# Branch A's logits: the product of the high parts in 64 rows of TensorE, two heads side by side, and the cross terms in 128 rows

## The chip, the cores and the metric

The kernel runs on one core of a Trainium2 chip. The metric is the device time of one execution in microseconds (us). Before the change three executions gave 1948.72, 1949.85 and 1950.54 us; the median is 1949.85 us. The execution that the profiler recorded took 1953.81 us, of which 1952.0 us lie between its first and its last instruction (the span).

The engines are named as in the profile: PE is TensorE (matrix products), PEld its weight loads, DVE is VectorE, ACT is ScalarE, POOL is GpSimd, SP is the queue that issues the DMAs.

## The reference

One encoder block over 2048 tokens of width 1024. An input projection feeds two attention mixers, A and B, whose outputs are gated, projected, merged and added to the residual. The change concerns the logits of mixer A, a window of 128 tokens to either side with 8 query heads of width 64 that share 2 key heads:

```python
qa = head_rms_norm(qa.reshape(bsz, S, A_Q_HEADS, HEAD_DIM), q_norm_a[layer]) * scale
ka = head_rms_norm(ka.reshape(bsz, S, A_KV_HEADS, HEAD_DIM), k_norm_a[layer])
...
scores = jnp.einsum('bnqkgd,bnmkd->bkgnqm', qb, kw).astype(jnp.float32)
...
logits = jnp.where(valid, scores + bias, NEG_INF)
```

Here a block of 128 queries meets the three blocks of 128 keys around it (two at either end of the sequence).

## The kernel before

**Numbers in two parts.** Products run in float16. An operand that needs more precision is split into a high part (the value rounded to float16) and a low part (what the rounding left, as float16). A product of two such operands is taken as high times high plus the cross terms high times low and low times high.

**Units.** The first part of the program works through 14 units, each a set of heads. Unit 0 and unit 2 belong to mixer A (4 query heads and 1 key head each), the other twelve to mixer B (2 heads each, one dilation). A unit has 8 pairs (`Pair`), each of which projects two blocks of 128 tokens onto the unit's query, key and value columns: 48 matmuls of line 632, in float16, into the tile `pj`. What a pair leaves in PSUM then goes through a chain of steps, among them `scale` (DVE, L692), `gain` (POOL, L699), `hi` (ACT, L705: the high parts of all normalised heads into the tile `spl`), `lo` (DVE, L709: the low parts), `swap` (POOL, L714: a copy of the key heads with their two parts exchanged) and `turn` (L722: one DMA transpose for each block, issued by SP, into the tile `kq`).

**The layout of `kq`.** `spl` holds for each token a list of slots of 128 columns, and each slot is one head: 64 columns of high parts, then 64 of low parts. After the transpose a slot has its 128 numbers over the 128 partitions, and so over the 128 rows of TensorE: high parts in partitions 0 to 63, low parts in 64 to 127. For a unit of A slots 0 to 3 are the query heads, slot 4 the key head (high over low) and slot 5 the same key head exchanged (low over high).

**Items.** An `Item` is one block of 128 queries with two heads (`h0` is 0 or 2 in A, so a block has two items). A unit of A has 32 items: 28 with three blocks of keys, 4 with two. In `logits` (L767) an item of A takes two of the three PSUM tiles `s`, one for each head, and for each head and each block of keys runs two matmuls in all 128 rows with the query slot as weights: against slot 4 (high times high and low times low, summed over the rows) and against slot 5 (both cross terms). That is 12 matmuls for three blocks of keys and 8 for two, each with its own weight load, each 128 columns wide. Then follow `maxima` (DVE, L797, one instruction for each head, which reads that head's `s` tile and takes the row's extreme value into `nmA`), `exps` (ACT, L805), `hi` (ACT, L810) and `lo` (DVE, L814) of the probabilities `p`, their DMA transpose into `pt` (L820) and `values` (PE, L831: 18 or 12 matmuls of 65 or 64 columns into `pv`).

**What sets the order.** The order on each engine is written by the program itself. `at` puts a step into a heap with a planned time, `until` emits whatever is due, and the main loop (L1077 on) emits the matmuls of line 632 one after another, with due steps between them. Planned times count in pairs; those of an item lie at fixed lags from its start (`LAGS`, `LV`), and items of A start a quarter of a pair apart. So in PE's queue an item's logits are one block of 12 matmuls among those of line 632, and the `values` of an older item follow a few matmuls later. Engines run their queues in order and wait for each other by semaphores.

Of the kernel before, what the change touches and what calls it, by code (L numbers as in the profile page):

```python
# [24 lines left out]
AF = mybir.ActivationFunctionType  # L25
OP = mybir.AluOpType
# [72 lines left out]
def block_kernel(tc, x, w_units, w_gate, w_mrg, w_out, w_bra, w_brk, gain, qkg, sink, bias_a, bias_b, b_merge, out):  # L99
    nc = tc.nc  # L100
    V = nc.vector
    A = nc.scalar
    G = nc.gpsimd
    T = nc.tensor
# [396 lines left out]
    def scale_time(t):  # L501
        return X_CH[0] + X_CH[1] * t
# [4 lines left out]
    for t in range(NT):  # L507
        b = X_SQ[0] + X_SQ[1] * t if t < 4 else X_SQ[2] + X_SQ[3] * (t - 4)
# [4 lines left out]
        b = scale_time(t)  # L513
        at(b, x_scale, t)
        for h in range(2):
            b = scale_time(t) + X_CH[2] + X_CH[5] * h
# [8 lines left out]
    for c in range(2):  # L525
        b = X_G[c]
# [88 lines left out]
    class Pair:  # L615
# [7 lines left out]
        def matmuls(self, i):  # L623
            un, (r, c) = self.un, self.subsets[i]
            self.ps[i] = ps = pj_p.tile([128, 512], F32, name="pj")
            out = []
            for a, b, aligned in ((0, 128, True), (128, 384, False)) if un.shift else ((0, 384, True),):
                h, lo = subset(0, un.g, r, c, aligned), subset(1, un.g, r, c, aligned)
                k = 0
                for ch in range(NCH):  # L630
                    for lhs, rhs in ((h, un.wh), (h, un.wl), (lo, un.wh)):
                        out.append(lambda lhs=lhs, rhs=rhs, ch=ch, a=a, b=b, k=k: T.matmul(  # L632
                            ps[:, a:b], lhsT=lhs[:, ch, :], rhs=rhs[:, ch, a:b], start=(k == 0), stop=(k == 23)))
                        k += 1
            return out
# [65 lines left out]
        def hi(self):  # L701

            n = 2 * self.nh
            self.q = self.rw[:, :n * HD].rearrange("p (s h e) -> p s h e", s=2, e=HD)
            A.activation(self.sp[:, :, :self.nh, 0, :], self.q, AF.Copy)  # L705

        def lo(self):
            sp, nh = self.sp, self.nh
            V.tensor_tensor(sp[:, :, :nh, 1, :], self.q, sp[:, :, :nh, 0, :], OP.subtract)  # L709

        def swap(self):
# [14 lines left out]
    class Item:  # L726
# [40 lines left out]
        def logits(self):  # L767
            un = self.un
            q = un.kq[(self.r, self.i)]
            if un.kind == "A":  # L770
                self.sv = [s_p.tile([128, 512], F32, name="s")[:, :self.W] for _ in range(2)]
            else:
                t = s_p.tile([128, 512], F32, name="s")
                self.sv = [t[:, self.W * j:self.W * j + self.W] for j in range(2)]
            for j in range(2):
                h = self.h0 + j
                kh = 0 if un.kind == "A" else h
                o = 0
                for s, k0, k1 in self.keys:
                    kt = un.kq[s]  # L780
                    for v in range(2):
                        T.matmul(self.sv[j][:, o:o + k1 - k0], lhsT=q[:, h, :],  # L782
                                 rhs=kt[:, un.nq + kh + v * un.nk, k0:k1], start=(v == 0), stop=(v == 1))
                    o += k1 - k0
# [290 lines left out]
    un, nxt = None, 0.0  # L1075
    t = 0
    while t < NPAIR or heap or any(k >= t for k in fill):  # L1077
        u, j = divmod(t, 8)
        steps = [(f, args) for f, *args in fill.pop(t, [])]
        if u < NU:  # L1080
            if j == 0:
                un = Unit(u)
# [5 lines left out]
            e = [t + 3.9 / (7.8 + 5.2 * len(steps)), t + 7.8 / (7.8 + 5.2 * len(steps))]  # L1088
# [86 lines left out]
    def s_build(q, ch):  # L1175
# [20 lines left out]
        def lo(j, k):  # L1196
            V.tensor_tensor(SL[q][:, j, ch, :], r[k][:], SH[q][:, j, ch, :], OP.subtract)

        return ((0, lambda: new(0, l21, l22, OP.add)), (1, lambda: new(1, h21, h22, OP.add)),
                (2, lambda: more(1, r[0][:], OP.add)), (2.1, lambda: hi(0, 1)),  # L1200
                (3, lambda: new(5, l11, l21, OP.subtract)), (4, lambda: new(3, h11, h21, OP.subtract)),
                (5, lambda: more(3, r[5][:], OP.add)), (5.1, lambda: hi(2, 3)), (6, lambda: lo(0, 1)),
                (7, lambda: new(2, r[1][:], h11, OP.subtract)), (8, lambda: more(2, l11, OP.subtract)),
                (8.1, lambda: hi(1, 2)), (9, lambda: lo(2, 3)),
                (10, lambda: new(4, h12, r[2][:], OP.subtract)), (11, lambda: more(4, l12, OP.add)),
                (11.1, lambda: hi(3, 4)), (12, lambda: lo(1, 2)), (13, lambda: lo(3, 4)))
# [297 lines left out]
    for dc, free in ((8, -2.3), (3, 0), (9, 2), (4, 4), (10, 6), (5, 8), (6, 10)):  # L1504
        ready += R8.get(dc, 0)
        b = max(first + GR * free + (WF if free > 0 else .3), ready + 22.0)
# [3 lines left out]
    b = max(ready, first + GR * 11)  # L1510
# [369 lines left out]
```

## Time and profile before

| | |
|---|---|
| median of 3 runs | 1949.85 us (1948.72 to 1950.54) |
| profiled execution | 1953.81 us, span 1952.0 us |
| PE busy | 1890.2 us, 97% of the span |
| DVE busy | 1483.1 us, 76% |
| ACT busy | 1241.1 us, 64% |
| POOL busy | 557.2 us, 29% |
| mean granted clock of TensorE | 0.994 of full speed |
| matmuls of L782 (logits of A and B) | 2016 weight loads, 148.7 us of PE busy time in one group of 1856 matmuls |

A time in the profile is counted from the start of the span. The time that a matmul is shown with is not the time that it keeps PE from the next one: matmuls are pipelined, the next starts long before the first has ended, and the end is modelled. What a matmul costs in a dense stretch is the distance from its start to the start of the next; what it shows as its duration is nearer to how long it takes from end to end. A row of the timeline merges equal instructions that follow each other (x12 is twelve), and its first number is the start of the first.

### The profile page before, as it was taken

Reading aid. Unit: us, or ns where it says so; the run is one execution under the profiler, and the core shown is the slowest. Engines: PE = TensorE matmul, PEld = TensorE weight load, DVE = VectorE, ACT = ScalarE, POOL = GpSimd, SP = SyncE. Lnnn points to the kernel's source line nnn. Section 1 sums busy time; section 2 is a strip of 40 time slices with the busy share of each in tenths; the row PEclk is TensorE's granted clock in tenths of the full one; section 3 lists DMA queues with packets and bytes.
Section 4 is the critical chain, followed back from the end, with each engine's and each line's share of the span. In section 5 each row is a group of like instructions: output and inputs, shape, how many; then the busy total and the mean of one; then the engine's idle time right before and its main releaser. Section 6 shows DMA issues by size and latency. Waiting matters only on the chain.

```text
span 1952.0 us, 51050 instructions
## 1 busy us (share of the span) xinstructions
PE 1890.2 (97%) x19302; PEld 1446.3 (74%) x19302; DVE 1483.1 (76%) x3777; ACT 1241.1 (64%) x2992; POOL 557.2 (29%) x1375
## 2 busy tenths in 40 slices
PE   4999999999999999999999999999999999999998
PEld 2567887889999899989999897544444445777774
DVE  5779888976896668866887768698877863987885
ACT  8577768886777667766776666465657675443341
POOL 1034343443553335433454334200000000222121
PEclk8999999999999999999999999999999999999999
DMA  6259988987888669877898578423666687754451
GB/s 240 64 108 192 175 179 138 187 163 152 165 152 180 132 126 192 148 145 154 136 177 154 99 124 161 117 71 110 187 197 192 181 270 256 264 154 135 139 157 63
DMA packets 631912, 309.18 MB, mean 158 GB/s; under 512 B 458480, under 2 KB 588656, under 8 KB 629232
## 3 DMA queue, kind: packets, MB, share of 16 engines
q1 hardware_dynamic: 631664, 305.92, 68.5%
q8 instruction: 151, 2.47, 0.5%
q14 instruction: 97, 0.79, 0.1%
HBM read 130.43 MB, written 65.27 MB: 100 GB/s over the span
## 4 chain that ended last, share of the span: by engine, by line
PE 80%; DVE 8%; DMA 6%; ACT 3%; issue 2%; SPq 1%; POOL 0%; DVEq 0%; POOLq 0%; ACTq 0%
PE pj L632 41%; PE fps L1385 9%; PE fps L1750 7%; PE fps L1678 6%; PE fps L294 5%; PE s L782 5%; PE pv L831 4%; PE pj L294 3%; DMA pt<-p 2%; DMA kq<-spl 2%; DVE wl L1287 1%; PE pt L895 1%; ACT jk L428 1%; DVE XL L1555 0%; DVE pr L797 0%
## 5 line engine op out<-in xcount | busy, mean ns | idle before, releaser
L632 PE MATMUL pj<-wl,XH 128*128 128x128 f16 (+2 forms) x2816 | 715.9, 268 | 0.0
L632 PE MATMUL pj<-wh,XL 128*128 128x128 f16 (+2 forms) x2816 | 712.3, 269 | 0.0
L632 PE MATMUL pj<-wh,XH 128*128 128x128 f16 (+2 forms) x2816 | 709.5, 268 | 0.0
L632 PEld LDWEIGHTS <-XH 128*128 128x128 f16 x5632 | 575.4, 112 | 54.6
L632 PEld LDWEIGHTS <-XL 128*128 128x128 f16 x2816 | 316.0, 112 | 24.1
L797 DVE CUSTOM_DVE_ANT_0 pr<-s,b,ubuf 128x256 f32<-128x256 f32 (+3 forms) x512 | 219.3, 466 | 70.3 <-PE s L782 66.9
L814 DVE SCALAR_TENSOR_TENSOR p<-pr,p 128x512 f16<-128x512 f32 (+2 forms) x256 | 194.8, 761 | 65.8 <-ACT p L810 62.9
L1688 POOL TENSOR_TENSOR g<-g,t 128x512 f32<-128x512 f32 x32 | 48.6, 1519 | 550.2 <-DMA g<-mgd 405.4
L699 POOL TENSOR_TENSOR rw<-rw,g 128x128 f32<-128x128 f32 (+1 forms) x224 | 136.4, 629 | 210.1 <-DVE rw L692 189.4
L650 ACT ACTIVATE rw<-pj 128x256 f32<-128x256 f32 (+1 forms) x224 | 87.4, 390 | 170.8 <-PE pj L632 170.1
L810 ACT ACTIVATE p<-pr 128x512 f16<-128x512 f32 (+2 forms) x256 | 157.7, 616 | 14.3 <-DMA pt<-p 9.7
L714 POOL COPY spl<-spl 128x256 f16<-128x256 f16 (+1 forms) x224 | 88.5, 425 | 257.6 <-DVE spl L709 257.6
L1678 PE MATMUL fps<-y,bigh 128*128 128x128 f16 x1792 | 153.7, 219 | 2.8 <-DVE r L1370 2.8
L782 PE MATMUL s<-kq 128*128 128x128 f16 (+1 forms) x1856 | 148.7, 218 | 6.8 <-DMA kq<-spl 5.7
L1750 PE MATMUL fps<-WO,mf 128*128 128x512 f16 x672 | 150.3, 379 | 2.4 <-DVE xr L1757 2.4
L1385 PEld LDWEIGHTS <-wh 128*128 128x128 f16 x784 | 76.8, 98 | 101.9 <-issue 11.7
L1678 PE MATMUL fps<-y,bigl 128*128 128x128 f16 x896 | 151.8, 219 | 0.0
L782 PEld LDWEIGHTS <-kq 128*128 128x128 f16 x2016 | 131.2, 98 | 23.2 <-issue 8.0
L1678 PEld LDWEIGHTS <-bigh 128*128 128x128 f16 x1792 | 139.2, 98 | 10.5 <-issue 3.2
L831 PE MATMUL pv<-vt,pt 128*128 128x65 f16 (+1 forms) x2784 | 132.1, 193 | 8.0 <-DMA pt<-p 8.0
L831 PEld LDWEIGHTS <-pt 128*128 128x128 f16 x3024 | 119.9, 98 | 23.9 <-DMA pt<-p 10.7
L1750 PEld LDWEIGHTS <-mf 128*128 128x128 f16 x672 | 64.5, 98 | 74.7 <-issue 2.8
(242 smaller groups left out, 3877.7 us busy)
## 6 DMA issues: line engine op xcount, KB each, us to landing
wraw<-in_w_units_dram SPq DMA_DIRECT2D x56, 384.0 KB, 4.8
g<-mgd SPq DMA_DIRECT2D x64, 256.0 KB, 4.6
mgd<-t SPq DMA_DIRECT2D x48, 256.0 KB, 2.3
wraw<-in_w_mrg_dram SPq DMA_DIRECT2D x44, 256.0 KB, 4.4
zd<-z SPq DMA_DIRECT2D x128, 66.0 KB, 2.0
zz<-zd SPq DMA_DIRECT2D x64, 132.0 KB, 3.2
xt<-in_x_dram SPq DMA_DIRECT2D x16, 512.0 KB, 10.0
ytd<-yo SPq DMA_DIRECT2D x32, 256.0 KB, 3.5
```

The costliest lines, as they stand in the source:

```text
L294: out.append(lambda w=w, xx=xx, ch=ch, i=i: T.matmul(ps[:], lhsT=w[:, ch, c0:c0 + 128], rhs=xx[:, ch, ts], start=(i == 0), stop=(i == n - 1)))
L632: out.append(lambda lhs=lhs, rhs=rhs, ch=ch, a=a, b=b, k=k: T.matmul(ps[:, a:b], lhsT=lhs[:, ch, :], rhs=rhs[:, ch, a:b], start=(k == 0), ...
L699: G.tensor_tensor(q[:, i, :un.nq, :], q[:, i, :un.nq, :], g, OP.mult)
L714: G.tensor_copy(sp[:, i, nh:, :, :], sp[:, i, nq:nh, ::-1, :])
L782: T.matmul(self.sv[j][:, o:o + k1 - k0], lhsT=q[:, h, :], rhs=kt[:, un.nq + kh + v * un.nk, k0:k1], start=(v == 0), stop=(v == 1))
L797: V.tensor_tensor_reduce(out=self.pv[:, j, self.p0:self.p0 + W], in0=self.sv[j], in1=un.bias[:, self.h0 + j, self.b0:self.b0 + W], scale=I ...
L810: A.activation(self.sp[:, :128 * n], self.pr, AF.Copy, scale=PSC)
L814: V.scalar_tensor_tensor(self.sp[:, 128 * n:], self.pr, PSC, self.sp[:, :128 * n], OP.mult, OP.subtract)
L831: T.matmul(self.po[:, j, :w], lhsT=p[:, n * j + s, :], rhs=un.v[key][:, vh, c0:c0 + w], start=(k == 0 and s == 0), stop=(k == 2 and s == n ...
L1385: out.append(lambda w=w, lo=lo, ch=ch, k=k: T.matmul(ps[:], lhsT=w[:, i, ch, :], rhs=xform(f, lo, ch, self.q), start=(fresh and k == 0), s ...
L1678: out.append(lambda p=p, c=c, wl=wl, yl=yl, n=n: T.matmul(ps[:, 128 * p:128 * p + 128], lhsT=w[wl][:, i, c, p, :], rhs=y[:, yl, c, :], sta ...
L1750: out.append(lambda p=p, ml=ml, wl=wl, k=k: T.matmul(ps[:], lhsT=m[:, ml, p, :], rhs=WO[:, i, wl, p, :], start=(fresh and k == 0), stop=(k ...
```

## The change

The units of A get a different layout for two of the four query heads, and a different set of products. Everything of B stays.

`hi` and `lo` now place the parts by the slot's parity: slots 0, 2 and 4 as before (high over low), slots 1 and 3 the other way round (low over high). Each of the two steps becomes two instructions, one for the even slots (3 heads in each of two blocks) and one for the odd (2 heads in each).

In `logits`, each head and block of keys now has one matmul in 128 rows for both cross terms: an even head (high over low) against slot 5 (low over high), an odd head (low over high) against slot 4 (high over low). High times high is a second matmul in 64 rows only: for the even head of the item rows 0 to 63 of its query slot and of slot 4, for the odd head rows 64 to 127 of its slot and of slot 5. These matmuls in 64 rows come after all the cross terms of the item, block of keys by block of keys, even head and odd head in turn. The products low times low are no longer taken. The number of matmuls is the same: 6 in 128 rows and 6 in 64 rows where there were 12 in 128 rows.

```diff
             n = 2 * self.nh
             self.q = self.rw[:, :n * HD].rearrange("p (s h e) -> p s h e", s=2, e=HD)
+            if self.un.kind == "A":
+                for o in range(2):
+                    A.activation(self.sp[:, :, o:5:2, o, :], self.q[:, :, o:5:2, :], AF.Copy)
+                return
             A.activation(self.sp[:, :, :self.nh, 0, :], self.q, AF.Copy)
 
         def lo(self):
             sp, nh = self.sp, self.nh
+            if self.un.kind == "A":
+                for o in range(2):
+                    V.tensor_tensor(sp[:, :, o:5:2, 1 - o, :], self.q[:, :, o:5:2, :], sp[:, :, o:5:2, o, :], OP.subtract)
+                return
             V.tensor_tensor(sp[:, :, :nh, 1, :], self.q, sp[:, :, :nh, 0, :], OP.subtract)
...
+            if un.kind == "A":
+                halves = []
+                for j in range(2):
+                    h, r = self.h0 + j, slice(64 * j, 64 * j + 64)
+                    o = 0
+                    for s, k0, k1 in self.keys:
+                        kt, out = un.kq[s], self.sv[j][:, o:o + k1 - k0]
+                        T.matmul(out, lhsT=q[:, h, :], rhs=kt[:, 5 - j, k0:k1], start=(o == 0), stop=False,
+                                 skip_group_check=True)
+                        o += k1 - k0
+                        halves.append((o, j, out, q[r, h, :], kt[r, 4 + j, k0:k1]))
+                for o, j, out, a, b in sorted(halves, key=lambda e: e[:2]):
+                    T.matmul(out, lhsT=a, rhs=b, start=False, stop=(o == self.W), skip_group_check=True)
+                return
             for j in range(2):
                 h = self.h0 + j
-                kh = 0 if un.kind == "A" else h
+                kh = h
```

How instructions move on PE: the logits of the first item of A that has three blocks of keys. Before, line 782 finishes the tile of the first head (`s_1210`) with its third block of keys (`kq_1137`) before it begins that of the second head (`s_1211`); `kq_1020` is the block of the queries and the middle block of keys, `kq_1018` the first block of keys.

```order
L782 LDWEIGHTS kq_1020
L782 MATMUL s_1210<-kq_1137,kq_1020 128x128
L782 LDWEIGHTS kq_1020
L782 MATMUL s_1211<-kq_1018,kq_1020 128x128
L782 LDWEIGHTS kq_1020
```

Now, for the same item, line 790 is a product in 128 rows and line 795 one in 64 rows; `s_1214` and `s_1215` are the tiles of the first and the second head, `kq_1022` the block of the queries, `kq_1020` and `kq_1141` the first and the third block of keys.

```order
L790 MATMUL s_1215<-kq_1141,kq_1022 128x128
L795 LDWEIGHTS kq_1022
L795 MATMUL s_1214<-kq_1020,kq_1022 128x128
L795 LDWEIGHTS kq_1022
L795 MATMUL s_1215<-kq_1020,kq_1022 128x128
L795 LDWEIGHTS kq_1022
L795 MATMUL s_1214<-kq_1022 128x128
```

Cross terms of both heads come first, then the products of the high parts switch from one head's tile to the other's at each step, so both tiles are finished only at the end of the block. The place of the block in PE's queue has not moved.

On DVE, in the second pair of unit 0, the one instruction for the low parts of both blocks has become two; what stands around it is the same.

```order
 L668 SCALAR_TENSOR_TENSOR vt<-pj,vt 128x64
 L692 TENSOR_TENSOR rw<-rw,qr 128x640
-L709 TENSOR_TENSOR spl<-rw,spl 128x2x5x64
+L715 TENSOR_TENSOR spl<-rw,spl 128x6x64
+L715 TENSOR_TENSOR spl<-rw,spl 128x2x2x64
```

ACT's instruction for the high parts is divided in the same way (L705 before, L707 now), and nothing else has moved on these engines.

## The prediction

> **What bounds the kernel now.** I read the timeline of PE around one item of A first, because it tells what a matmul costs, then the table of windows over the two stages in which A's items run, then the waits there.
>
> ```profile
> start us, us, engine line op out<-in xcount [idle before <-releaser]
> 122.05 0.83 PE L782 MATMUL s<-kq 128*128 128x128 f16 x12
> 122.72 0.33 PE L632 MATMUL pj<-wh,XL 128*128 128x384 f16 x1
> ...
> 123.20 0.53 PE L831 MATMUL pv<-vt,pt 128*128 128x65 f16 x12
> 123.57 0.32 PE L632 MATMUL pj<-wh,XL 128*128 128x384 f16 x1
> ```
>
> Twelve logit matmuls start at 122.05 and the next projection at 122.72: 0.67 us, 56 ns each, weight load included. The twelve matmuls of 65 columns behind them take 0.37 us, 31 ns each, so a weight load and a short matmul together can follow each other that fast. PE has no gap here, and what it charges for is columns.
>
> The stages: A's first unit has its items from 113 to 226 us, the second from 312 to 405 us. In the rows below each engine's busy time stands in the order PE, PEld, DVE, ACT, POOL, then the granted clock and the DMA share.
>
> ```profile
> 113.00:140.00 27.00, 26.87 (x272) 18.76 (x270) 22.08 (x57) 21.85 (x48) 8.19 (x24) 1.00 0.50 94
> 140.00:170.00 30.00, 28.31 (x377) 21.06 (x375) 28.80 (x73) 25.79 (x60) 13.86 (x27) 1.00 0.90 155
> 170.00:200.00 30.00, 28.21 (x448) 26.16 (x447) 28.60 (x72) 23.10 (x54) 11.23 (x22) 1.00 1.19 218
> 200.00:226.00 26.00, 23.68 (x359) 22.41 (x360) 20.11 (x56) 20.07 (x49) 7.25 (x16) 0.93 1.02 179
> 312.00:350.00 38.00, 38.00 (x490) 28.48 (x489) 36.44 (x87) 35.20 (x81) 14.60 (x31) 1.00 0.86 143
> 350.00:380.00 30.00, 29.52 (x387) 24.41 (x385) 28.20 (x72) 24.91 (x58) 12.77 (x24) 1.00 1.07 197
> 380.00:405.00 25.00, 23.73 (x307) 21.02 (x305) 20.89 (x55) 21.66 (x52) 8.98 (x21) 1.00 1.11 203
> ```
>
> PE is not alone. From 140 to 200 us DVE is busy 57.40 of 60 us and from 312 to 380 us 64.64 of 68 us, 95% both times, while PE stands idle for 3.5 and 0.5 us. Over both stages:
>
> ```profile
> 113.00:226.00 113.00, 107.07 (x1451) 88.39 (x1449) 99.58 (x254) 90.81 (x210) 40.54 (x89) 0.98 0.91 163
> 312.00:405.00 93.00, 91.24 (x1176) 73.91 (x1175) 85.53 (x213) 81.77 (x189) 36.35 (x76) 1.00 0.99 177
> ```
>
> PE is idle for 5.9 us in the first and 1.8 us in the second. The chain that ended last shows for what:
>
> ```profile
> 184.28 5.78 DMA pt<-p
> 190.06 0.05 issue
> 190.10 0.53 PE pv L831 x12
> 190.63 6.42 DMA pt<-p
> ...
> 202.91 6.44 DMA pt<-p
> ...
> 346.41 5.03 DMA pt<-p
> ...
> 379.02 5.68 DMA pt<-p
> ...
> 387.36 4.86 DMA pt<-p
> ```
>
> These are the transposes of probabilities that DVE and ACT delivered late. Time won or lost on PE ahead of such a wait changes first the wait, and the end only by what is left.
>
> **The change, part by part.** How many items there are I take from the row maxima, one instruction for each head; these rows are the groups of the first stage.
>
> ```profile
> L797 DVE CUSTOM_DVE_ANT_0 pr<-s,b,ubuf 128x384 f32<-128x384 f32 x56 | 32.2, 613 | 4.0 <-PE s L782 3.3
> L797 DVE CUSTOM_DVE_ANT_0 pr<-s,b,ubuf 128x256 f32<-128x256 f32 x8 | 3.5, 480 | 2.4 <-PE s L782 2.4
> ```
>
> 28 items with three blocks of keys and 4 with two: 92 blocks of keys for a unit, 184 for both, with four matmuls each before.
>
> *Overlap of the halves.* Now each block has two cross matmuls (112 ns) and a pair in 64 rows. If the two of a pair run side by side, the pair costs at least one matmul's 56 ns and, as two loads and two matmuls at 31 ns, 62 ns. A block goes from 223 to 173 ns: 50 ns won, 9.2 us over 184 blocks, 4.6 us for a stage. The other bound is no overlap: 56 ns each, nothing won. I take the overlap, since the two use different rows, partitions and PSUM tiles.
>
> *Switching between 128 and 64 rows.* Each item goes into 64 rows once and back once: 64 items, 128 switches. No row shows such a switch. The lower bound is another kind of switch, from float16 products to float32 transposes:
>
> ```profile
> 176.21 0.22 PE L632 MATMUL pj<-wl,XH 128*128 128x128 f16 x1
> 176.26 0.61 PE L895 MATMUL pt<-idf,ya 128*128 128x128 f32 x4
> 176.71 0.22 PE L632 MATMUL pj<-wh,XL 128*128 128x128 f16 x1
> ```
>
> The transposes start 0.05 us behind a product, which is its ordinary 56 ns: that switch is free. The upper bound is that nothing overlaps across the border, neither the products nor the next weight load.
>
> ```profile
> L782 PEld LDWEIGHTS <-kq x2016: 95/98/147, 113.1 to 1228.1; 128*128 128x128 f16 x184
> L782 PE MATMUL s<-kq x1856: 192/219/311, 113.2 to 1228.0; 128*128 128x128 f16 x178, 128*128 128x64 f16 x8
> ```
>
> A matmul takes 219 ns from end to end and costs 56 in a stream: 163 ns are lost if the next waits for its end, 261 with the 98 ns of the load. I take 163 ns. The transposes use the array as one piece, as everything in this trace does; sums that leave the array halfway down and sums that run through all of it should not be under way together, while weights for the next product can still be brought in. 128 times 163 ns is 20.9 us. PE's own bill is then 20.9 - 9.2 = +11.7 us, 5.85 us for a stage.
>
> The Trainium skill has a rule on either side here. "TensorEngine Tiling (Array Packing)", Key Properties, says that changing the tiling mode drains TensorE and that changing only the tile does not; it gives no price, and with a drain priced by the rows above the sum is the one I make. "TensorE: Matmul & The Clock Gate", Part 3, says that matmuls in different row groups run at once with some 4 ns between their starts; by that figure alone, without a drain, PE would win an estimated 9.5 us. No trace here shows either.
>
> *The split into high and low parts.* 16 pairs of A now run two instructions where one ran, on ACT and on DVE.
>
> ```profile
> L705 ACT ACTIVATE spl<-rw 128x512 f16<-128x512 f32 x96 | 60.3, 628 | 57.2 <-POOL vt L661 51.5 <-POOL rw L699 5.0
> L705 ACT ACTIVATE spl<-rw 128x640 f16<-128x640 f32 x16 | 11.7, 729 | 8.6 <-POOL vt L661 8.6
> ...
> L709 DVE TENSOR_TENSOR spl<-rw,spl 128x512 f16<-128x512 f32 x96 | 66.0, 687 | 2.1 <-ACT spl L705 2.1
> L709 DVE TENSOR_TENSOR spl<-rw,spl 128x640 f16<-128x640 f32 x16 | 13.1, 821 | 3.5 <-ACT spl L705 3.5
> ```
>
> From 512 to 640 elements ACT adds 101 ns and DVE 134 ns, so without elements there remain 224 ns on ACT and 151 ns on DVE: 3.6 and 2.4 us in all, half for a unit. ACT's lies beside other work (its highest share in the windows is 93%). DVE's 1.2 us for a unit falls on the engine that is 95% busy; where PE sets the end, PE's longer item hides it, and where DVE does, it counts in full. The key heads come 0.4 us later for their transpose; no row of these stages shows PE waiting for `kq`, and that cover is worth the same 0.4 us for each pair if it is gone. POOL's copy (L714) is the same, and SP issues the same transposes.
>
> *The first head's row maxima.* Its tile was ready after half of the block, now almost at its end, 0.15 to 0.5 us later, and behind that maximum stand the second head's and all of DVE's queue. DVE waited for logits only a few times (the two rows of maxima: 5.7 us in the first stage, 2.4 of it at its first items), for it is mostly behind. I count it inside the first term below.
>
> *The sum.* First stage: until 140 us DVE still waits for PE, and 6 of the 32 items lie there, so 6/32 of 5.85, 1.1 us, pass on to DVE's chain, and DVE's own 1.2 us stand behind it; the rest of PE's 5.85 us goes into the 5.9 us in which it waits now. +2.3 us. Second stage: 5.85 less the 1.8 us of idle time, with DVE's 1.2 us beside it: +4.1 us. Together +6.4 us, the profiled execution from 1953.8 to 1960.2 us. That execution lies 4.0 us above the median, so the median goes to 1956 us. If all idle time took its share and DVE's 2.4 us hid, it would be +4; if none did, +11.7.
>
> **The rivals.** *The overlap without a price for the switch.* For it speaks the free switch to the transposes. PE wins 9.2 us, but DVE holds most of it: from 312 to 380 us it needs 64.64 and some 1.0 of its new 1.2 us, so of these 68 us at most 2.4 can go; from 380 to 405 DVE is free and PE's 1.0 us (7 of 32 items) counts; in the first stage 0.9 us ahead of 140 us counts against DVE's 1.2 us. In all -3 us, 1947, between -9 (all of PE's gain arrives) and 0. More waiting may also cost clock, as the 0.93 granted from 200 to 226 us hints.
>
> *A dearer switch.* At 261 ns, load and all, the switches cost 33.4 us, PE's bill is +24.2, and after 5.9 and 1.8 us of idle time and the 1.1 us passed on it comes to some +17 us, 1967. It decides from some 220 ns a switch. Halves that do not overlap at 163 ns a switch give +13, 1963. For them: weight loads end within 98 ns at best, and nothing in the trace has them in half the rows. Against: all loads in the trace hide.
>
> *It does not do what it says.* The halves follow one another and a switch costs nothing: PE's bill is nought, DVE's 2.4 us counts in part, +1.5 us, 1951.
>
> **How the numbers follow.** Chances: the forecast 0.45, the overlap without a price 0.31, the dearer switch (or no overlap) 0.14, no effect on PE 0.10. The time is that of the forecast, 1956. The range goes from 1945.5, which leaves out the best quarter of the second case, to 1966, which leaves out the upper half of the third; the forecast's own range is 1953 to 1962. A change of 0.2%, 3.9 us, is about what a measurement can tell from none. Faster by more: half of the overlap's case and a trace of the forecast, 0.17. Slower by more: 0.36 of the forecast's 0.45, the dearer switch's 0.14 and 0.02 of the last, 0.52. Within: the remaining 0.31.
>
> **What would show it.** In the timeline of an item of three blocks, six matmuls of line 790 at 56 ns, then a gap of some 0.16 us ahead of line 795, starts of line 795 in pairs nearly together or at about 31 ns, and another gap ahead of the next projection: about 0.85 us from the first logit to that projection, where it was 0.67. With the free switch it is 0.52, with the dear one 1.04. The waits of PE for `pt` should shrink in the first stage; in the first rival they grow. L707 and L715 should show some 220 and 150 ns more for a pair together than one instruction did. I am wrong about the switch if an item takes 0.67 us or less, and about who sets the end if an item's change times 64 comes out in the total undiminished.

## The result, and the profile after

The changed kernel took 1956.85 us (median of 5 runs, 1954.98 to 1959.89), the kernel before, beside it, 1950.54 us (1948.72 to 1951.72). The ratio is 1.0030 with a 95% interval of 1.0017 to 1.0043. In a second session, beside the first experiments, it was 1956.78 us against 1952.11 us, ratio 1.0019 (1.0010 to 1.0028). The change makes the kernel slower, by 0.2 to 0.3%.

The two profiled executions are less far apart than that, 1953.2 us of span against 1952.0: the one of before was slower than all five runs timed here, the one of after the fastest of its five. So the profiles are read below for what happens in one place, and the ratios for the size of the whole.

The item whose twelve logit matmuls took 0.67 us before, in the timeline of PE after the change (start, duration, engine, line, operation, tiles, shapes, count):

```profile
122.24 0.33 PE L632 MATMUL pj<-wl,XH 128*128 128x384 f16 x1
122.40 0.50 PE L790 MATMUL s<-kq 128*128 128x128 f16 x6
122.83 0.34 PE L795 MATMUL s<-kq 64*128 64x128 f16 x6
123.11 0.34 PE L632 MATMUL pj<-wh,XL 128*128 128x384 f16 x1
123.28 0.33 PE L632 MATMUL pj<-wh,XH 128*128 128x384 f16 x1
```

Six products in 128 rows would take 0.34 us at 56 ns; the products in 64 rows start 0.43 us after them, so 0.10 us are lost on the way in. Three pairs at 56 ns would take 0.17 us; the next projection starts 0.28 us after them, and 0.10 us are lost on the way out. Single records of the trace show the two matmuls of a pair starting 3 to 4 ns apart. From the first logit to the next projection it is 0.705 us, where it was 0.670. An item with two blocks of keys takes 0.537 us, where it took 0.447.

The weight loads of the same products:

```profile
122.24 0.48 PEld L790 LDWEIGHTS <-kq 128*128 128x128 f16 x6
122.83 0.17 PEld L795 LDWEIGHTS <-kq 64*128 64x128 f16 x6
```

The loads for line 790 begin 0.16 us ahead of their first product, those for line 795 together with theirs. So nothing is loaded during the 0.10 us. Whether these are the time until the products ahead are through, or a weight load that for once is not hidden (92 to 98 ns shown), the runs do not separate.

The two stages, in the order PE, PEld, DVE, ACT, POOL, clock, DMA share:

```profile
113.00:226.00 113.00, 107.18 (x1441) 83.05 (x1439) 99.78 (x257) 90.83 (x213) 41.10 (x89) 0.98 0.92 162
312.00:405.00 93.00, 91.19 (x1146) 67.67 (x1145) 84.37 (x215) 80.93 (x191) 37.41 (x76) 1.00 0.95 170
```

PE's idle time is what it was, 5.8 and 1.8 us; a second profile of the changed kernel has 6.0 and 1.6. Its waits for `pt` in the first stage went from 6.2 to 5.5 us. The divided steps, in the groups of DVE and ACT:

```profile
L715 DVE TENSOR_TENSOR spl<-rw,spl 128x384 f16<-128x384 f32 x16 | 8.9, 553 | 2.8 <-ACT spl L707 2.8
L715 DVE TENSOR_TENSOR spl<-rw,spl 128x256 f16<-128x256 f32 x16 | 6.7, 416 | 0.0
...
L707 ACT ACTIVATE spl<-rw 128x384 f16<-128x384 f32 x16 | 8.3, 516 | 8.7 <-POOL vt L661 8.7
L707 ACT ACTIVATE spl<-rw 128x256 f16<-128x256 f32 x16 | 6.4, 402 | 0.0
```

On DVE 553 + 416 = 969 ns for a pair stand where 821 stood, on ACT 918 where 729 stood: 148 and 189 ns more, 2.4 and 3.0 us over 16 pairs.

How long a stage lasts is read best from an instruction that belongs to A alone, the read of the row maxima into `nmA`, 64 in each stage. Its rows name the first and the last start; here those of before, first stage and second:

```profile
L797 DVE DVE_READ_ACCUMULATOR2_ANT nmA<- x64: 76/83/86, 114.0 to 225.5; 128x1 f32 x64
L797 DVE DVE_READ_ACCUMULATOR2_ANT nmA<- x64: 79/83/86, 308.2 to 409.5; 128x1 f32 x64
```

and of after:

```profile
L819 DVE DVE_READ_ACCUMULATOR2_ANT nmA<- x64: 77/82/88, 114.4 to 226.7; 128x1 f32 x64
L819 DVE DVE_READ_ACCUMULATOR2_ANT nmA<- x64: 76/83/86, 308.8 to 412.4; 128x1 f32 x64
```

The first stage went from 111.5 to 112.3 us, the second from 101.3 to 103.6 us: +0.8 and +2.3. These are single executions. The second profile of the changed kernel has 112.7 and 103.3 us; a kernel that takes as long as the one before, the one below with its PSUM divided another way, has 110.4 and 103.0. So one stage alone can be off by 1 to 2 us, while the two together differ less: 212.8 and 213.4 us for these two kernels, 215.9 and 216.0 for the changed one.

### The profile page after: what moved, and what is told of

Read it like the earlier page. It is cut to its first block, busy times and chain, and to the rows that moved or that the text cites. A ratio compares the mean times of both kernels' runs of the same rounds, so it can differ in the third digit from the quotient of the medians.

```text
span 1953.2 us, 51082 instructions
## 1 busy us (share of the span) xinstructions
PE 1894.0 (97%) x19302; PEld 1437.3 (74%) x19302; DVE 1485.0 (76%) x3793; ACT 1243.1 (64%) x3008; POOL 559.9 (29%) x1375
## 4 chain that ended last, share of the span: by engine, by line
PE 80%; DVE 10%; DMA 4%; ACT 3%; issue 2%; POOL 0%; SPq 0%; DVEq 0%; ACTq 0%; POOLq 0%
PE pj L632 42%; PE fps L1407 8%; PE fps L1772 7%; PE fps L1700 6%; PE fps L294 4%; PE pv L853 4%; PE s L804 3%; PE pj L294 3%; DMA pt<-p 2%; DMA kq<-spl 1%; DVE wl L1309 1%; DVE pr L819 1%; PE pt L917 1%; PE s L790 1%; DVE y L1651 1%
## 5 line engine op out<-in xcount | busy, mean ns | idle before, releaser
L804 PE MATMUL s<-kq 128*128 128x128 f16 (+1 forms) x1120 | 96.0, 218 | 5.3 <-DMA kq<-spl 5.3
L827 ACT ACTIVATE pr<-pr,z 128x128 f32<-128x128 f32 (+2 forms) x256 | 98.8, 440 | 0.8 <-DVE z L819 0.7
```

Source lines behind the costliest of these rows:

```text
L804: T.matmul(self.sv[j][:, o:o + k1 - k0], lhsT=q[:, h, :], rhs=kt[:, un.nq + kh + v * un.nk, k0:k1], start=(v == 0), stop=(v == 1))
L827: A.activation(v, v, AF.Exp, bias=self.stat(j), scale=-1.0)
```

## The experiments

PE's own bill for the change is now known: 56 items at 35 ns and 8 at 90 ns, 2.7 us, and 10 to 52 ns (15 in the mean) at the first projection behind each of the 64 items, 3.6 us together. Three theories of what makes the end later were set against each other. Theory 1: PE's longer items and DVE's extra work bring a part each. Theory 2: the divided steps bring nearly all, and PE's bill goes into its waits. Theory 3: the first head's tile, which is ready later, brings nearly all.

**The changed kernel once more**, for the sessions that follow.

> The changed kernel once more, beside the three that follow. All theories: between 3 and 8 us above the kernel before; an item of A with three blocks of keys takes 0.705 us on PE, one with two 0.537.

Measured: the 1.0019 above, +3.7 us (2.0 to 5.5, from the interval and the 1952 us of before).

**The divided steps alone.**

```diff
+            if self.un.kind == "A":
+                for o in range(2):
+                    A.activation(self.sp[:, :, o:5:2, o, :], self.q[:, :, o:5:2, :], AF.Copy)
+                return
...
+            if self.un.kind == "A":
+                for o in range(2):
+                    V.tensor_tensor(sp[:, :, o:5:2, 1 - o, :], self.q[:, :, o:5:2, :], sp[:, :, o:5:2, o, :], OP.subtract)
+                return
```

> The new layout with its two instructions for the high and two for the low parts, but all logit products in 128 rows and in the old order, so an item takes 0.670 us on PE. Theory 1 (PE's longer items and DVE's extra work each bring a part): +1 to +2.4 us over the kernel before. Theory 2 (the divided steps on ACT and DVE bring nearly all, PE's bill goes into its waits): +5 to +7 us. Theory 3 (the late tile of the first head brings nearly all): 0 to +1 us.

Measured: ratio 1.0007 (0.9998 to 1.0016), +1.4 us (-0.4 to +3.1); an item at 0.670 us. Theory 2 falls, since its lower end is 5.

**The new products alone.** The same lines taken out of the changed kernel.

> The new products and their order, with the old layout and one instruction each for the high and low parts; the odd heads' logits so lack the product of the query's high and the key's low part (and have low times low). An item takes 0.705 us on PE. Theory 1: +3 to +5 us. Theory 2: 0 to +1 us. Theory 3: +5 to +7 us.

Measured: ratio 1.0014 (1.0006 to 1.0023), +2.7 us (1.2 to 4.5); an item at 0.705 us. The two parts, 1.4 and 2.7, add up to 4.1 where the whole is 3.7. That fits theory 1, though 2.7 lies a little under its range; theory 3's lower end of 5 lies outside the interval, and so does theory 2's +1. This kernel also has the changed order of the products, so the 2.7 us belong to PE's bill and to the order together.

**The products in 64 rows first.**

```diff
+                for o, j, out, a, b in sorted(halves, key=lambda e: e[:2]):
+                    T.matmul(out, lhsT=a, rhs=b, start=(o == 0), stop=False, skip_group_check=True)
+                for out, a, b, stop in cross:
+                    T.matmul(out, lhsT=a, rhs=b, start=False, stop=stop, skip_group_check=True)
```

> The changed kernel with the products in 64 rows ahead of the cross terms, so the first head's tile is ready after 9 of 12 products, not 11; the switch into 64 rows follows a projection of 384 or 128 columns, not a logit product. Theory 1: within 1.5 us of the changed kernel; an item again near 0.70 us from the end of the last projection to the start of the next if a switch costs what is under way beyond the columns. Theory 3: 2 to 5 us faster than the changed kernel. If the price of a switch grows with the columns of the product ahead of it, the first switch costs some 100 ns more, 6 us in all on PE.

Measured: ratio 1.0019 (1.0010 to 1.0028), the same as the changed kernel; no gain from the earlier tile shows, and theory 3's 2 to 5 us are missing. The timeline of PE:

```profile
122.39 0.33 PE L632 MATMUL pj<-wl,XH 128*128 128x384 f16 x1
122.65 0.34 PE L794 MATMUL s<-kq 64*128 64x128 f16 x6
122.92 0.51 PE L796 MATMUL s<-kq 128*128 128x128 f16 x6
123.27 0.33 PE L632 MATMUL pj<-wh,XL 128*128 128x384 f16 x1
```

Here the way in follows a projection of 384 columns, which keeps PE for 0.16 us: the halves start 0.26 us after it, again 0.10 us late, and the way out of three pairs again takes 0.27 us. The price of a border does not grow with the columns of the product ahead of it.

**Four borders instead of two in each item.**

```diff
+                        late = o > 0
+                        prods.append((late, 0, j, o, out, q[:, h, :], kt[:, 5 - j, k0:k1], o == 0, False))
+                        o += k1 - k0
+                        prods.append((late, 1, o, j, out, q[r, h, :], kt[r, 4 + j, k0:k1], False, o == self.W))
+                for *_, out, a, b, start, stop in sorted(prods, key=lambda e: e[:4]):
+                    T.matmul(out, lhsT=a, rhs=b, start=start, stop=stop, skip_group_check=True)
```

> The changed kernel with two excursions into 64 rows in each item (the pair of the first block of keys behind its two cross terms, the other pairs at the end), the same products. Theory 1 (each border between 128 and 64 rows costs the same, 96 ns or so, whatever stands around it): an item of three blocks takes 0.90 us on PE instead of 0.705, one of two 0.73 instead of 0.537; 12.3 us more on PE, of which the first stage's waits take up to 5.8 and the second's 1.8: +5 to +9 us over the changed kernel. Rival (a first border is dear, later ones are not, or the end does not follow PE at all): within 2 us of the changed kernel.

Measured: 1961.32 us, ratio 1.0043 (1.0030 to 1.0056); over its own kernel before that is 9.7 us by the medians, where the changed kernel had 4.7: +5.0, the lower edge. (The two intervals leave it between some 2 and 8.) An item takes 0.92 us (0.75 with two blocks):

```profile
122.39 0.33 PE L632 MATMUL pj<-wl,XH 128*128 128x384 f16 x1
122.55 0.99 PE L795 MATMUL s<-kq 128*128 128x128 f16 x12
123.47 0.34 PE L632 MATMUL pj<-wh,XL 128*128 128x384 f16 x1
```

(The view merges both kinds into one row here, since they have one line.) Two more borders cost 0.21 us: every border has its price. Where the time went, in the same rows of `nmA`:

```profile
L819 DVE DVE_READ_ACCUMULATOR2_ANT nmA<- x64: 76/83/86, 114.4 to 225.6; 128x1 f32 x64
L819 DVE DVE_READ_ACCUMULATOR2_ANT nmA<- x64: 73/83/84, 308.8 to 416.4; 128x1 f32 x64
```

Against before PE has 8.2 us more to do in each stage (28 items at 0.248 us and 4 at 0.303). The first stage lasts 111.2 us, no longer than before. The second lasts 107.6 us, 6.3 us longer, which is the bill less the 1.8 us in which PE stood idle.

**Both heads' halves in the same rows.**

```diff
-                        halves.append((o, j, out, q[r, h, :], kt[r, 4 + j, k0:k1]))
+                        halves.append((o, j, out, q[0:64, h, :], kt[0:64, 4, k0:k1]))
```

> The old layout with one instruction each for the high and low parts; the products of the high parts in 64 rows, but of both heads in rows 0 to 63, one after the other. If the overlap of two row halves is what makes a pair cheap, each product costs 56 ns again and an item of three blocks takes 0.86 us, one of two 0.64: 9.6 us more on PE than with the pairs side by side, +4 to +8 us over the kernel that had the new products without the divided steps. Rival (a product in 64 rows is cheap by itself): 0.70 us and no difference.

Measured: 1958.05 us, ratio 1.0031 (1.0020 to 1.0041), 6.4 us over its kernel before by the medians; the kernel with the new products alone had 3.5. +3 us, a little less than expected, with intervals of 1.6 us and more on either number. PE:

```profile
123.13 0.50 PE L782 MATMUL s<-kq 128*128 128x128 f16 x6
123.56 0.51 PE L787 MATMUL s<-kq 64*128 64x128 f16 x6
124.00 0.34 PE L632 MATMUL pj<-wh,XL 128*128 128x384 f16 x1
```

The same six products in 64 rows, now all in one half, take 0.44 us to the next projection instead of 0.28, while the way in is the same 0.43. A product in 64 rows is not cheaper by itself; what makes it cheap is a partner in the other rows.

**Twice as many pairs between two borders, and the same products in 128 rows.** Each product of the high parts is issued twice, so the logits hold them double; the second kernel differs in this line:

```diff
-                        halves.append((o, j, out, q[r, h, :], kt[r, 4 + j, k0:k1]))
+                        halves.append((o, j, out, q[:, h, :], kt[:, 4 + j, k0:k1]))
```

> The changed kernel with every product of the high parts issued twice (the high parts count double in the logits), so that one excursion into 64 rows holds twice as many pairs. If a pair saves 52 ns and the two borders cost 192: an item of three blocks takes 0.86 us on PE, one of two 0.64. To be read against the next kernel, 128 rows for the same products: 8 us less on PE, 0 to 6 us faster at the end, so that the sign turns with the number of pairs between two borders. Rival (the borders' price grows with what they enclose): 0.95 us or more, no faster than the next.

> As the kernel before this one, in the new layout and with the same order of products, but the products of the high parts in all 128 rows (so low times low is in them too), each issued twice: 18 products of 56 ns, 1.00 us for an item of three blocks, 0.67 for one of two, no borders.

Measured: 1957.55 us (ratio 1.0030, 1.0019 to 1.0041) in 64 rows and 1964.69 us (1.0066, 1.0054 to 1.0078) in 128 rows. Here the 64 rows are 7.1 us faster, more than the 6 expected at most, though the intervals reach down to 4. On PE, 64 rows first, then 128:

```profile
122.54 0.50 PE L790 MATMUL s<-kq 128*128 128x128 f16 x6
122.97 0.51 PE L795 MATMUL s<-kq 64*128 64x128 f16 x12
123.41 0.34 PE L632 MATMUL pj<-wh,XL 128*128 128x384 f16 x1
```

```profile
122.96 0.50 PE L790 MATMUL s<-kq 128*128 128x128 f16 x6
123.30 0.83 PE L795 MATMUL s<-kq 128*128 128x128 f16 x12
123.97 0.33 PE L632 MATMUL pj<-wh,XL 128*128 128x384 f16 x1
```

Six pairs take 0.87 us with their item, 18 products in 128 rows 1.005: 0.133 us won, where three pairs lost 0.035. So each further pair wins 56 ns, two borders cost 203 ns, and an excursion into 64 rows pays from four pairs on. Over 56 items at 0.133 and 8 at 0.021 us that is 7.6 us on PE, of which 7.1 arrived. In the kernel with 128 rows PE has 10.3 us more than before in each stage, and hardly waits in either. Its stages:

```profile
L820 DVE DVE_READ_ACCUMULATOR2_ANT nmA<- x64: 77/83/85, 114.9 to 227.7; 128x1 f32 x64
L820 DVE DVE_READ_ACCUMULATOR2_ANT nmA<- x64: 77/83/86, 309.2 to 418.1; 128x1 f32 x64
```

112.8 and 108.9 us: 1.3 us longer in the first stage, 7.6 us in the second. The first stage swallows nearly the whole of a PE bill, the second passes most of it on. It swallows more than the 5.9 us of idle time, because idle time counts too little: a matmul that is shown with 219 ns and costs 56 covers up to 163 ns of a wait behind it. Counted from start to start, beyond what the products' columns cost in a stream (an estimate from single records), PE waits some 9.5 us in the first stage and 3.1 in the second before the change, and about 1 us in each in the kernel with 128 rows.

**The order alone.** Both tiles ready late, all products in 128 rows, old layout.

> The kernel before with the order of the changed one alone: old layout, one instruction each for the high and low parts, all products in 128 rows, but the cross terms of both heads first and then the other products of the two heads in turn, so both tiles are ready only at the end of an item. An item stays at 0.670 us on PE. Theory 1: -1 to +1 us against the kernel before. Theory 3 (the late tile of the first head): +2 us or more.

Measured: ratio 1.0007 (0.9998 to 1.0016), +1.4 us (-0.4 to +3.1), between the two expectations. With the earlier tile of the halves-first kernel worth nothing, theory 3 has no support as the main cause; whether the order costs a microsecond stays open. The lengths of the two stages, added up from the first and last starts of `nmA`, say how it might divide: 212.8 us before, 213.9 with the order alone, 214.1 with the divided steps alone, 214.6 with the new products and their order, 215.9 for the whole. By these single executions the order could be over half of what the new products bring; with 0.6 us between two kernels that take the same time, that isn't settled.

**One excursion for two items.** The trace says what could beat the kernel before: six pairs between two borders, from the two items of a block. That needs four logit tiles, and room for the fourth is made by putting the two tiles of the values side by side in one. First that division alone:

```diff
-    s_p = main.enter_context(tc.tile_pool(name="sp", bufs=3, space=PSUM))
+    s_p = main.enter_context(tc.tile_pool(name="sp", bufs=4, space=PSUM))
...
-    pv_p = main.enter_context(tc.tile_pool(name="pv", bufs=2, space=PSUM))
+    pv_p = main.enter_context(tc.tile_pool(name="pv", bufs=1, space=PSUM))
+    pvt, pvn = pv_p.tile([128, 2, 2, 72], F32, name="pv"), [0]
...
-            self.po = pv_p.tile([128, 2, 72], F32, name="pv")
+            self.po = pvt[:, pvn[0] % 2]
+            pvn[0] += 1
```

> The kernel before with its PSUM divided another way: four tiles for logits instead of three, the two tiles of the values side by side in one tile. Nothing else. To be read with the next kernel. All theories: -1 to +1 us against the kernel before.

Measured: ratio 1.0001 (0.9992 to 1.0010). PE does have a new wait in the second stage, for the shared tile of the values:

```profile
PE pv L833 <- ACT zz L852: 1.4, 1, 1.4
```

Then with the changed kernel's products for two items:

```diff
+                for it in its:
+                    for j in range(2):
...
+                            halves.append((it.h0, o, j, out, q[r, h, :], kt[r, 4 + j, k0:k1]))
+                for _, o, j, out, a, b in sorted(halves, key=lambda e: e[:3]):
+                    T.matmul(out, lhsT=a, rhs=b, start=False, stop=(o == self.W), skip_group_check=True)
```

> The changed kernel on that PSUM, with the logits of a block's two items taken together: twelve cross products, then six pairs, one excursion into 64 rows for four heads. If a pair saves 52 ns and an excursion costs 192: 1.21 us for both items of three blocks of keys (before: 1.34), 0.88 for two of two (before: 0.89), 3.8 us less on PE than the kernel before; the divided steps give 1 to 2 us back and DVE, which is nearly full, holds part: -3 to +2 us against the kernel before, 2 to 6 us faster than the changed kernel. Rival (what counts is not the number of borders): no faster than the changed kernel.

Measured: ratio 1.0010 (1.0001 to 1.0019), +1.9 us against the kernel before, 1.8 us faster than the changed one by the ratios, which their intervals do not tell from nothing. PE does what was expected, 1.21 us for two items:

```profile
122.17 0.83 PE L796 MATMUL s<-kq 128*128 128x128 f16 x12
122.93 0.51 PE L801 MATMUL s<-kq 64*128 64x128 f16 x12
123.38 0.34 PE L633 MATMUL pj<-wh,XL 128*128 128x384 f16 x1
```

But PE now waits longer in the second stage. The longest of the waits in PE's queue there (time in total, times, longest):

```profile
PE pv L860 <- ACT zz L879: 2.3, 1, 2.3
PE pv L860 <- DMA pt<-p: 1.6, 3, 0.8
```

and the stage:

```profile
312.00:405.00 93.00, 88.73 (x1158) 68.15 (x1156) 85.08 (x218) 81.01 (x192) 35.66 (x76) 1.00 0.97 172
```

PE is idle for 4.3 us of the same 93, where it was 1.8 before and 3.3 with the PSUM divided this way and nothing else. One last kernel took the divided steps out of this one:

> The kernel with one excursion for a block's two items, with the old layout and one instruction each for the high and low parts; the odd heads' logits so lack the product of the query's high and the key's low part. PE as in that kernel, 1.21 us for two items of three blocks of keys. If the divided steps are what keeps the 4 us won on PE from showing: -2 to 0 us against the kernel before. If DVE, full in these stages without them too, or the shared tile of the values holds it: +1 to +3 us, as in that kernel.

Measured: ratio 1.0002 (0.9993 to 1.0011), +0.4 us (-1.4 to +2.1), which the intervals don't tell from either expectation. No gain shows, though PE has 3.8 us less to do in its items; its idle time in that window is 3.9 us, with one wait of 2.2 us for the shared tile of the values. What holds the gain, DVE or that tile, these kernels do not separate. No version beat the kernel before.

## Why the prediction was right, and where not

**The side and the size.** Slower, 1956 us forecast, 1956.85 and 1956.78 us measured; +6.4 us forecast, +6.3 by the medians of the first session and +4.7 of the second (by the second's ratio +3.7, and its interval, 2.0 to 5.5, leaves the forecast out). The size is better than the working deserved, because of two errors that offset each other in part; that much of it is luck.

**The overlap** was right. A pair costs 56 ns, a little less than the 62 ns that the sum took, and the kernel with both halves in the same rows shows that the partner is the reason. "TensorE: Matmul & The Clock Gate", Part 3, in the Trainium skill, says that matmuls in different row groups run at once, started some 4 ns apart. The trace agrees, with 3 to 4 ns.

**The price of a switch** was there, and mis-sized: 163 ns, from a matmul's end-to-end time less its cost in a stream, where two borders cost 203 ns, some 100 each. The first product behind a border starts 0.15 us after the start of the last one ahead of it, so it does not wait for the end that the profile shows after 0.22 us. The prediction also let the next weights come in meanwhile; the loads show that they do not, and what the 0.10 us are made of stays open. So PE's bill was 3.6 us, not 11.7. The Trainium skill, "TensorEngine Tiling (Array Packing)", Key Properties, says that a change of tiling mode drains TensorE; the trace agrees in that each border costs 0.10 us, in either direction, and does not show that draining is the reason. The rival without a price for the switch is out, and so is the dearer one.

**The divided steps** were right on DVE (151 ns forecast, 148 measured) and near on ACT (224 and 189). They were said to vanish beside PE's longer items in the second stage. Whether they do is not shown: alone they bring +1.4 us, with an interval that just reaches zero, and beside the new products 1.0 us more, which the intervals do not tell from nothing.

**The sum over the stages** is where the second error lay. It let the first stage take +2.3 us and the second +4.1, out of 5.85 us of PE's bill each. With bills of that size the step holds in the second stage: four borders (8.2 us a stage) gave +6.3 us there, both halves in the same rows 5.0 us for a bill of 6.4. In the first stage it asks too much: for four borders its working gives some +3.5 us, and the profile shows -0.3, since PE waited more there than the idle time says. With the real bill of 1.8 us a stage it would have given about 1.5 us in the first stage and between nothing and DVE's 1.2 in the second, and the profile shows +0.8 and +2.3. The idle time of 1.8 us was hardly used up by the small delay: after the change it is still 1.8 us, 1.6 in the second profile, 1.4 with the new products alone. A reason could be that what PE waits for comes a little later too, since DVE, at 95%, has more to do and gets its logits later; no run shows this. How the second stage's part divides between PE, DVE and the order was not separated; the two single experiments give 1.4 and 2.7 us of the whole.

**The first head's tile** was counted as part of the first term. The order alone gave +1.4 us (-0.4 to +3.1), so it can be nothing or a good part of the new products' 2.7; the earlier tile of the halves-first kernel brought no gain.

**The rival that the change doesn't do what it says** is out by the timeline. An item's change times 64 (3.6 us) came out undiminished in the end (3.7 to 5.9 us by the two ratios, with what the divided steps and the order bring), which the prediction named as the sign that it was wrong about who sets the end. For so small a bill it may have been; without the other two parts the runs do not say how much of the 3.6 us arrived.

## What to carry to other kernels

Products in half of the rows pay only in company: a pair in the two halves costs one product, but each change between 128 and 64 rows costs about 0.10 us here, so gather at least four pairs of 128 columns between two changes, or leave it. That wins time on PE only: six pairs between two changes won 0.13 us for two items and nothing in the end. Before pricing the step, count how many changes the surrounding order forces; here each item of three pairs paid two. And where two engines are both above 90% busy, do not charge a small delay against the idle time that the profile shows: large bills used it up and more, beside the small one it stayed nearly what it was.

## What the runs showed of the hardware

In these kernels the price of a border does not depend on how long the product ahead of it is: 0.10 us behind one of 384 columns as behind one of 128, and the same in both directions. It is less than the 163 ns by which a matmul's shown time of 219 ns exceeds its 56 ns in a stream. The weight loads of the halves (92 to 96 ns shown) are hardly shorter than those of 128 rows (95 to 98 and more), and in the pairs both loads hide all the same.
